# Regrouping attention rows: blocks of 32 rows of four heads, keys to the block's end, operands laid out through DRAM

## Chip, cores and metric

One NeuronCore of a Trainium2 (trn2) runs the whole kernel. The metric is the device time in microseconds of one execution; lower is better. Engines: PE is TensorE (matmuls and transposes), DVE is VectorE, ACT is ScalarE, POOL is GpSimd, SP is SyncE, which only issues DMAs.

## The reference, cut to what matters

A layer over 512 rows of width 1024. One projection gives the inputs of two attentions of 8 heads each (two groups of four heads share a key/value head); `n` is the first, with three branches that share a query, and `d` the second. Both normalise and rotate queries and keys.

```python
h = rms_norm(x, norm_gain)
proj = jnp.einsum('bsd,dc->bsc', h, w_in)
...
o_cmp, p_cmp = compressed_branch(qn, kc_cmp, vc_cmp)   # 31 compressed keys, masked by block end
o_sel = selected_branch(qn, ks_r, vs, sel_idx)         # 16 blocks wanted, 8 there are: every causal key
o_win = window_branch(qn, kw_r, vw)                    # window 512 of 512 rows: every causal key
o_nsa = g[..., 0:1] * o_cmp + g[..., 1:2] * o_sel + g[..., 2:3] * o_win
...
score = jnp.einsum('bths,bth->bts', relu(logits), wi)  # indexer
_, idx = lax.top_k(score, 128)
o_dsa = ...                                            # softmax over the 128 keys kept, causal
mixed = jnp.concatenate([o_nsa * silu(z_n), o_dsa * silu(z_d)], axis=-1)
return x + jnp.einsum('bsc,cd->bsd', mixed, w_out)
```

## The kernel before

**Tiling.** The 512 rows are four tiles of 128 (`NT = 4`). The projection runs in chunks of columns (I, C, B, Q1, Q2, D, Z0 to Z3); every product of float32 operands is three products of fp32r parts, hi·hi, hi·lo and lo·hi. ACT makes the hi part (L354), POOL most lo parts (L355). The constants, one DRAM tensor `cst`, are loaded near the start; POOL's first operation needs them.

**Attention.** A unit is one branch of one row tile i and group g, named `n{i}{g}{branch}` (1 selected, 2 window, 0 compressed) or `d{i}{g}0`. For each head h of the group the transposed queries of the tile, 128 rows, are the stationary operand, and the first 128(i + 1) keys move past them, in two products (hi and lo of the key) into one PSUM bank (`scores_of`, L964; names `s_n301` and so on, and `sc_` for the compressed branch alone). Then, in `softmax_of`:

- DVE adds the mask, multiplies by the row's norm factor `u.r` and takes the minimum, in one pass out of PSUM (L945; the page calls it CUSTOM_DVE_ANT_0);
- ACT exponentiates and sums (L947), DVE takes the reciprocals after the fourth head (L949), POOL multiplies by the gate (L951) and normalises each head (L959).

The probabilities are transposed by PE, 128 columns at a time (L999), split by ACT and DVE (L1000, L1001), and multiplied with the values (L1010). `combine` puts the four heads' outputs together. `qstack` makes the stationary queries out of the rotated ones (two transposes, L602, a copy by ACT, a subtraction by DVE, L608).

**Factors and masks.** The queries aren't normalised: `norm_of` (L562) turns sums of squares into factors `rs` by a chain of small POOL operations (`rsqrt`, L414 to L421), [row, tile × head], and the reduction applies them. The indexer's top 128 come from 16 passes MAX8 / MATCH_REPLACE of DVE (L671, L672) for each of the tiles 3, 2 and 1; POOL turns what was replaced into a mask (L674) that the `d` units of that tile use.

**Order.** `weave` mixes the attention's steps with fill work for PE (Q2, D and Z chunks, the output projection). At the end `set_order` orders every engine's instructions anew, the DMA queue of SP among them, by modelled costs and due times; `CHOICE` is one of its weights. PSUM has two banks for scores (`S`), so a third score product waits until the softmaxes of the first have read its bank. `AHEAD` is the number of units whose probabilities are kept ahead of their transposes.

Of the kernel before, what the change touches and what calls it, by code (L numbers as in the profile page):

```python
# [9 lines left out]
F32 = mybir.dt.float32  # L10
F32R = mybir.dt.float32r
# [44 lines left out]
C_VALID = C_CMASK + NT * 32  # L56
C_CCOS = C_VALID + 2
# [4 lines left out]
ARENA = 2824 + 1536 + 256 + 512 - 768 - 1024  # L62
# [6 lines left out]
TBUFS, AHEAD, LAG = 3, 3, 2  # L69
# [29 lines left out]
CHOICE = 0.25  # L99
# [208 lines left out]
def tile_hybrid_layer(ctx, tc, xT, x, ng, win, gains, peT, w1, b1, w2, wout, cst, out):  # L308
# [6 lines left out]
    psum = ctx.enter_context(tc.tile_pool(name="psum", bufs=2, space=PSUM))  # L315

# [186 lines left out]
    cmask = cs[:, C_CMASK:C_CMASK + NT * 32].rearrange("p (t c) -> p t c", t=NT)  # L503
    valid = cs[:, C_VALID:C_VALID + 1]
# [39 lines left out]
    def norm_scale(Rs_, ss):  # L544
# [7 lines left out]
        rsqrt(y, af, NT * n, div=HD, magic=MAGIC + 3 * 2.0 ** 23)  # L552
# [802 lines left out]
```

## Time and profile before

| | |
|---|---|
| median of 3 runs | 317.41 us (316.76 to 317.8) |
| profiled execution, its own time | 317.49 us |
| its span in the trace | 315.7 us |
| busy: PE, DVE, ACT, POOL | 310.4, 260.1, 243.7, 242.3 us |
| DMA moved | 30.26 MB, mean 96 GB/s |

The span runs from the first to the last instruction in the trace; the profiled execution's time has 1.8 us around it. Busy time of an engine is the time in which at least one of its instructions ran. The chain that ended last is followed backwards from the last instruction to what released each step.

### The profile page before, as it was taken

The page shows a single profiled execution, that of the slowest core. Times are in us where ns is not written, and L with a number is a line of the kernel's source. Part 1 is how long each engine was busy: PE and PEld are TensorE (multiplying, and loading weights), DVE is VectorE, ACT ScalarE, POOL GpSimd, SP SyncE. Part 2 cuts the span into 40 slices and gives each one's busy share as a digit, 9 for nine tenths or more (in the row PEclk, how much of TensorE's full clock was granted, in tenths as well). Part 3 has the DMA queues.
Part 4 walks back from the last instruction along what each step waited for, and adds up shares of the span by engine and source line. Part 5 has one row for each costly group of instructions (what it writes and reads, how often), then busy time and mean ns, then how long its engine had stood idle before and what let it go on. Part 6 is the DMA issues. An engine that isn't in the chain of part 4 may idle for free.

```text
span 315.7 us, 5949 instructions
## 1 busy us (share of the span) xinstructions
PE 310.4 (98%) x1693; PEld 261.6 (83%) x1693; DVE 260.1 (82%) x773; ACT 243.7 (77%) x791; POOL 242.3 (77%) x416
## 2 busy tenths in 40 slices
PE   8999999999999999999999999999999999999995
PEld 5988888998868888888888888888888888888885
DVE  4997523889899999999999999999998989896401
ACT  6962765989899899989999999663559997996400
POOL 2099989997995399989998988795859997757500
PEclk9999999999999999999999999999999999999999
DMA  7990455544610034100150124030426324004011
GB/s 287 395 315 3 122 154 160 163 138 123 167 48 0 2 95 132 44 1 0 30 139 1 36 69 131 3 105 28 135 67 165 104 63 137 3 0 136 0 66 66
DMA packets 14944, 30.26 MB, mean 96 GB/s; under 512 B 1792, under 2 KB 2176, under 8 KB 14912
## 3 DMA queue, kind: packets, MB, share of 16 engines
q1 hardware_dynamic: 14912, 29.90, 31.1%
q8 instruction: 13, 0.21, 0.3%
q14 instruction: 19, 0.16, 0.2%
HBM read 27.79 MB, written 2.10 MB: 95 GB/s over the span
## 4 chain that ended last, share of the span: by engine, by line
PE 90%; ACT 2%; POOL 2%; issue 2%; DMA 1%; DVE 1%; DVEq 0%; POOLq 0%; ACTq 0%
PE z L398 14%; PE out L1178 14%; PE on L1010 7%; PE B L388 7%; PE D L388 7%; PE s_n L964 6%; PE T_n L999 6%; PE Q L388 5%; PE I L477 5%; PE C L398 4%; PE s_d L964 3%; PE od L1010 3%; PE T_d L999 3%; PE qT_ps L602 1%; PE I L441 1%
## 5 line engine op out<-in xcount | busy, mean ns | idle before, releaser
L947 ACT ACTIVATE P_n<-P_n,arena 128x512 f32<-128x512 f32 (+3 forms) x64 | 36.0, 565 | 3.4 <-DVE arena L945 2.9
L945 DVE CUSTOM_DVE_ANT_0 P_n<-s_n,arena 128x512 f32<-128x512 f32 (+3 forms) x64 | 34.0, 543 | 0.4
L959 POOL TENSOR_SCALAR P_n<-P_n,arena 128x512 f32<-128x512 f32 (+3 forms) x64 | 33.1, 535 | 1.1
L964 PE MATMUL s_n<-kn,arena_r 128*128 128x512 f32 (+4 forms) x112 | 29.8, 348 | 0.5 <-DVE arena_r L608 0.5
L1001 DVE TENSOR_TENSOR ptl<-T_n,pth 128x512 fp32r<-128x512 f32 x40 | 27.4, 686 | 1.1 <-ACT pth L1000 0.5
L671 DVE MAX8 m<-scores 128x8 f32<-128x512 f32 (+2 forms) x48 | 26.6, 553 | 0.4
L672 DVE MATCH_REPLACE8 scores<-m,scores 128x512 f32<-128x512 f32 (+2 forms) x48 | 26.1, 544 | 0.1
L398 PE MATMUL z<-hThi,whi_Z 128*128 128x512 f32 x64 | 26.1, 411 | 0.0
L398 PE MATMUL z<-hTlo,whi_Z 128*128 128x512 f32 x64 | 25.3, 398 | 0.0
L398 PE MATMUL z<-hThi,wlo_Z 128*128 128x512 f32 x64 | 25.2, 397 | 0.0
L999 PE MATMUL T_n<-arena,P_n 128*128 128x128 f32 x160 | 25.2, 272 | 0.0
L1000 ACT CAST pth<-T_n 128x512 fp32r<-128x512 f32 x40 | 23.3, 581 | 2.4 <-PE T_n L999 2.3
L1178 PE MATMUL out<-whi_wo,mx 128*128 128x512 f32 (+1 forms) x72 | 24.6, 381 | 0.0
L1178 PE MATMUL out<-wohi,mx 128*128 128x512 f32 (+1 forms) x72 | 24.1, 378 | 0.0
L964 PEld LDWEIGHTS s_n<-kn,arena_r 128*128 128x128 f32 x112 | 20.0, 188 | 4.7 <-DVE arena_r L608 0.9
L999 PEld LDWEIGHTS T_n<-arena,P_n 128*128 128x128 f32 x160 | 20.0, 140 | 4.6
L355 POOL TENSOR_TENSOR wlo_Z<-raw_Z,whi_Z 128x512 fp32r<-128x512 f32 x16 | 20.5, 1297 | 3.8 <-ACT whi_Z L354 3.8
L388 PE MATMUL Q<-whi_Q,hThi 128*128 128x256 f32 (+1 forms) x64 | 22.1, 345 | 0.0
L388 PE MATMUL Q<-wlo_Q,hThi 128*128 128x256 f32 (+1 forms) x64 | 22.0, 347 | 0.0
L388 PE MATMUL Q<-whi_Q,hTlo 128*128 128x256 f32 (+1 forms) x64 | 21.7, 341 | 0.0
L355 POOL TENSOR_TENSOR w1l<-raw_w,w1h 128x512 fp32r<-128x512 f32 x16 | 20.6, 1293 | 1.2 <-DMA raw_w<-in_w_dram 1.1
L947 ACT ACTIVATE P_d<-P_d,arena 128x512 f32<-128x512 f32 (+3 forms) x32 | 17.9, 560 | 3.1 <-DVE arena L945 3.1
(262 smaller groups left out, 1105.8 us busy)
## 6 DMA issues: line engine op xcount, KB each, us to landing
raw_w<-in_w_dram SPq DMA_DIRECT2D x16, 256.0 KB, 2.9
raw_Z<-in_win_dram SPq DMA_DIRECT2D x16, 256.0 KB, 2.8
wor<-in_wout_dram SPq DMA_DIRECT2D x16, 256.0 KB, 2.8
raw_Q<-in_win_dram SPq DMA_DIRECT2D x12, 256.0 KB, 2.8
raw_D<-in_win_dram SPq DMA_DIRECT2D x8, 256.0 KB, 2.7
xres<-in_x_dram SPq DMA_DIRECT2D x8, 256.0 KB, 2.8
out_dram<-xres SPq DMA_DIRECT2D x7, 256.0 KB, 2.0
xw<-in_xT_dram SPq DMA_DIRECT2D x2, 860.0 KB, 8.0
```

Of the source, the lines that this page charges most:

```text
L355: engine.tensor_tensor(lo, raw, hi.bitcast(F32), op=ALU.subtract)
L388: nc.tensor.matmul(out_ps, a[:, k, tsl], b, start=(k == 0 and b is hi and a is hT["hi"]), stop=(k == KB - 1 and a is hT["lo"]))
L398: nc.tensor.matmul(out_ps, b[:, csl], a[:, k, :], start=(k == 0 and b is hi and a is hT["hi"]), stop=(k == KB - 1 and b is lo))
L671: nc.vector.max(m8, sc)
L945: nc.vector.tensor_tensor_reduce(P[:, h], src_, mask, u.r[:, h:h + 1], 3e38, op0=ALU.add, op1=ALU.min, accum_out=m[:, h:h + 1])
L947: nc.scalar.activation(P[:, h], P[:, h], AF.Exp, bias=m[:, h:h + 1], scale=-1.0, accum_out=l[:, h:h + 1])
L959: nc.gpsimd.tensor_scalar(P[:, hh], P[:, hh], l[:, hh:hh + 1], 1.0 if u.gate is not None else 0.5, op0=ALU.mult, op1=ALU.mult)
L964: nc.tensor.matmul(p, q[:, h, :], k[:, x], start=(x == 0), stop=(x == 1))
L999: nc.tensor.transpose(p[:, h * 128:(h + 1) * 128], u.P[:, h, j * 128:(j + 1) * 128], ident)
L1001: nc.vector.tensor_tensor(pl, p, ph.bitcast(F32), op=ALU.subtract)
L1010: nc.tensor.matmul(o, u.v[j], pp, start=(u.first and j == 0 and x == 0), stop=(end and x == 1))
L1178: nc.tensor.matmul(p, a, b[:, csl], start=(k == 0 and b is hi and a is mx[0]), stop=(k == 7 and a is mx[1]))
```

## The change

The rows of a score product are regrouped. Before, a product had 128 rows of one head; after, it has 32 rows of each of the group's four heads (block b of the tile, b = 0 to 3, in place of head h), so that only the keys up to the block's end, `keys(b)` = 128i + 32b + 32, have to move, be masked, exponentiated and normalised. Everything that is held per row has to follow that layout: [32·head + row in block, block] instead of [row, head].

- `qstack` writes the queries in blocks (the indexer keeps the old form), and `combine` reads the outputs so.
- The gates, the norm factors of q and d and the three masks go to DRAM and come back in four reads each (`by_blocks`): 8 writes and 32 reads. With two copies of the first 128 window keys (needed beside the other keys of tile 0) these are 42 more DMAs, all issued by SP.
- The mask is made by ACT (Relu with a large bias) instead of POOL.
- Transposes still take whole 128-column tiles, so DVE sets to zero the last 96 columns of blocks 0 to 2 in each of the 24 wide units (all but the compressed ones).
- A unit of kind `d` of tiles 0 and 1 no longer widens its product to 256 columns. The compressed keys share a product with the selected ones where both fit in 512 columns.
- `AHEAD` goes from 3 to 2, `CHOICE` from 0.25 to 0; POOL makes one small constant more; buffers change size.

```diff
-ARENA = 2824 + 1536 + 256 + 512 - 768 - 1024
+ARENA = 3689
...
-TBUFS, AHEAD, LAG = 3, 3, 2
+TBUFS, AHEAD, LAG = 3, 2, 2
...
-CHOICE = 0.25
+CHOICE = 0.0
...
+    trib = carve([S], BF16)
+    nc.gpsimd.memset(trib, 0.0)
+    nc.gpsimd.tensor_copy(trib[:, S - 32:], cs[:, C_TRIB:C_TRIB + 32])
...
-        rsqrt(y.rearrange("p t h -> p (t h)"), af, NT * nh, magic=MAGIC - 2.0 ** 31)
+        rsqrt(z, af, NT * 4)
+        by_blocks(y, z.rearrange("p (h t) -> p h t", t=NT), name)
...
+        if blocks:
+            pv = p[:, :256].rearrange("p (a b r) -> p a b r", a=2, b=4)
+            qv = q.rearrange("p b (a e r) -> p e a b r", a=2, e=2)
...
+    def by_blocks(dst, src_, name):
+
+        n = src_.shape[-1]
+        scr = dram.tile([128, 4 * n], F32, tag="dr_" + name, name="dr_" + name)
+        nc.sync.dma_start(scr, src_.rearrange("p h n -> p (h n)"))
+        v = scr.rearrange("(b r) (h n) -> r h b n", b=4, h=4)
+        for h in range(4):
+            nc.sync.dma_start(dst[32 * h:32 * h + 32], v[:, h])
...
-            mbias[i] = b8.tile([128, n], BF16, tag=f"masks{i}", name=f"masks{i}")
-            nc.gpsimd.tensor_scalar(mbias[i], sc, -2e38, NEG, op0=ALU.is_gt, op1=ALU.mult)
+                nc.vector.match_replace(sc, m8, sc, -3e30)
+            mk = b8.tile([128, n], BF16, tag=f"masks{i}", name=f"masks{i}")
+
+            nc.scalar.activation(mk, sc, AF.Relu, bias=big)
+            mbias[i] = dram.tile([128, n], BF16, tag=f"dr_mask{i}", name=f"dr_mask{i}")
+            nc.sync.dma_start(mbias[i], mk)
...
+            if b:
+                for k in kn:
+                    nc.sync.dma_start(k[:, :, K_WIN0:K_CMP].bitcast(F32), k[:, :, 0:128].bitcast(F32))
...
+        P, m, l = u.P[:, b, :n], u.m, u.l
+        nc.vector.tensor_tensor_reduce(P, src_, mask, u.r[:, b:b + 1], 3e38, op0=ALU.add, op1=ALU.min,
+                                       accum_out=m[:, b:b + 1])
+        if b == 0 and u.P.shape[-1] > 32:
+
+            nc.vector.memset(u.P[:, 0:3, u.P.shape[-1] - 96:], 0.0)
+        nc.scalar.activation(P, P, AF.Exp, bias=m[:, b:b + 1], scale=-1.0, accum_out=l[:, b:b + 1])
...
-                for hh in range(4):
-                    nc.gpsimd.tensor_scalar(P[:, hh], P[:, hh], l[:, hh:hh + 1], 1.0 if u.gate is not None else 0.5,
+                for bb in range(4):
+                    Pb = u.P[:, bb, :128 * u.i + 32 * bb + 32]
+                    nc.gpsimd.tensor_scalar(Pb, Pb, l[:, bb:bb + 1], 1.0 if u.gate is not None else 0.5,
...
-    def scores_of(p, q, h, k):
-        for x in range(2):
-            nc.tensor.matmul(p, q[:, h, :], k[:, x], start=(x == 0), stop=(x == 1))
-
-    def softmax_steps(k, parts):
-
-        u = parts[0][0]
-        n = k.shape[-1]
-        for h in range(4):
-            p = ps("S", "s_" + u.name)[:, :n]
-            scores_of(p, u.q[0], h, k)
-            for v, cols, mask in parts:
-                softmax_of(v, h, p[:, cols], mask)
-            yield 2 * COST * n
-
-    def compressed_steps(u, k, mask):
-        p = ps("S", "sc_" + u.name)
-        for h in range(4):
-            scores_of(p[:, 32 * h:32 * h + 32], u.q[0], h, k)
-        for h in range(4):
-            softmax_of(u, h, p[:, 32 * h:32 * h + 32], mask)
-        yield 0.86
+    def softmax_steps(q, products):
+
+        for b in range(4):
+            for k, parts in products(b):
+                n = k.shape[-1]
+                p = ps("S", "s_" + parts[0][0].name)[:, :n]
+                for x in range(2):
+                    nc.tensor.matmul(p, q[0][:, b], k[:, x], start=(x == 0), stop=(x == 1))
+                for v, cols, mask in parts:
+                    softmax_of(v, b, p[:, cols], mask)
+                yield 2 * COST * max(n, 256)
...
+        keys = lambda b: 128 * i + 32 * b + 32
+        causal = lambda b: trib[:, S - keys(b):]
...
+            if g == 0 and i:
+
+                mm = work.tile([128, 4, n], BF16, tag="mm", name=f"mm{i}", bufs=2)
+                v = mbias[i].rearrange("(b r) n -> r b n", b=4)
+                for h in range(4):
+                    nc.sync.dma_start(mm[32 * h:32 * h + 32], v)
+                ST["mm", i] = mm
+            u.S = lambda: softmax_steps(q, lambda b: [
+                (ST["kdi"][:, g, :, :keys(b)], [(u, slice(0, keys(b)), ST["mm", i][:, b, :keys(b)] if i else causal(b))])])
...
-            us.S = lambda: softmax_steps(k[:, :, w0:K_SEL + n], [sel(n + 32), win_, cmp(n)])
+            us.S = lambda: softmax_steps(q, lambda b: [
+                (k[:, :, K_WIN0:K_SEL + 128], [sel(b, 160), win_(b), cmp(b, 128)])])
         else:
-            uw.S = lambda: softmax_steps(k[:, :, w0:S], [win_])
-            if i < 3:
-                us.S = lambda: softmax_steps(k[:, :, K_CMP:K_SEL + n], [sel(32), cmp(0)])
-            else:
-                us.S = lambda: softmax_steps(k[:, :, K_SEL:], [sel(0)])
-                uc.S = lambda: compressed_steps(uc, k[:, :, K_CMP:K_SEL], cmask[:, i, :])
+            uw.S = lambda: softmax_steps(q, lambda b: [(k[:, :, 0:keys(b)], [win_(b)])])
+            us.S = lambda: softmax_steps(q, lambda b: [
+                (k[:, :, K_CMP:K_SEL + keys(b)], [sel(b, 32), cmp(b, 0)])] if keys(b) + 32 <= 512 else [
+                (k[:, :, K_SEL:], [sel(b, 0)]), (k[:, :, K_CMP:K_SEL], [cmp(b, 0)])])
```

How the order changes, at three places. The first is PE at the first score products (`s_n301`, tile 3, group 0, selected branch; `Q2_*` are projection products, `hid1` the compression's). Before:

```order
L964 MATMUL s_n301_1489<-kn0_385,arena_r_71 128x512 [waits DVE_49]
L964 MATMUL s_n301_1489<-kn0_385,arena_r_71 128x512
L388 MATMUL Q2_1_1466<-wlo_Q22_1087,hThi_72 128x512
L388 MATMUL Q2_1_1466<-whi_Q22_1086,hTlo_73 128x512
L388 MATMUL Q2_1_1466<-whi_Q23_1096,hThi_72 128x512
L388 MATMUL Q2_1_1466<-wlo_Q23_1097,hThi_72 128x512
L757 MATMUL hid1_1321<-arena_70,scr_1320 128x64 x2
L964 MATMUL s_n301_1498<-kn0_385,arena_r_71 128x512 [waits DVE_49,PE_49]
L964 MATMUL s_n301_1498<-kn0_385,arena_r_71 128x512
```

and after, where the lines are L1010 for score products, L390 for projections:

```order
L790 MATMUL hid1_1345<-arena_72,scr_1344 128x64 [waits DVE_49]
L790 MATMUL hid1_1345<-arena_72,scr_1344 128x64
L1010 MATMUL s_n301_1528<-kn0_397,arena_r_73 128x448 [waits DVE_49]
L1010 MATMUL s_n301_1528<-kn0_397,arena_r_73 128x448 [waits Activation_49]
L1010 MATMUL s_n301_1540<-kn0_397,arena_r_73 128x480 x2
L390 MATMUL Q2_2_1615<-whi_Q20_1083,hThi_74 128x512 [waits DVE_49,PE_49]
L390 MATMUL Q2_2_1615<-wlo_Q20_1084,hThi_74 128x512
L390 MATMUL Q2_2_1615<-whi_Q20_1083,hTlo_75 128x512
L390 MATMUL Q2_2_1615<-whi_Q20_1083,hThi_74 128x512
L390 MATMUL Q2_2_1615<-wlo_Q20_1084,hThi_74 128x512
L390 MATMUL Q2_2_1615<-whi_Q20_1083,hTlo_75 128x512
L1010 MATMUL s_n301_1550<-kn0_397,arena_r_73 128x512 [waits PE_49]
```

Before, the first score products stand between the Q2 products of row tile 1, one head at a time, two of four heads in these rows. Now all of Q2's tile 1 comes before them, blocks 0 and 1 follow at once with 448 and 480 columns (the 32 compressed keys are in them), and block 2 waits for the bank behind six products of tile 2.

The second is DVE at the first softmax. Before (L945 the reduction, L672 an indexer pass, ISA without shape names the readout of the minimum):

```order
L672 MATCH_REPLACE scores3_558<-m8_597,scores3_558 128x512 [waits DVE_49]
L945 ISA P_n301_1492,arena_70<-s_n301_1489,arena_70 128x512 [waits PE_49,Pool_49]
L945 ISA arena_70 128x1
L945 ISA P_n301_1492,arena_70<-s_n301_1498,arena_70 128x512 [waits PE_49]
L945 ISA arena_70 128x1
L671 MAX m8_597<-scores3_558 128x8 [waits DVE_49]
```

and after (L982 the reduction, L986 the zeroing):

```order
L701 MATCH_REPLACE scores_391<-m8_608,scores_391 128x512 [waits DVE_49]
L982 ISA P_n301_1531,arena_72<-s_n301_1528,arena_72 128x416 [waits DMAHW5_49,DMAHW4_49,DMAHW6_49,DMAHW3_49,PE_49]
L982 ISA arena_72 128x1
L986 MEMSET P_n301_1531 128x3x96
L982 ISA arena_72<-s_n301_1528,arena_72 128x32
L982 ISA arena_72 128x1
L982 ISA P_n301_1531,arena_72<-s_n301_1540,arena_72 128x448 [waits DVE_49,PE_49]
L982 ISA arena_72 128x1
L982 ISA arena_72<-s_n301_1540,arena_72 128x32
L982 ISA arena_72 128x1
```

The first reduction waited for PE and POOL, and now waits for PE and for four DMA lanes; each block has two reductions, 416 or 448 wide and 32 wide, and the zeroing stands behind the first.

The third is SP's queue, where the factors of q0 go out and come back. Before, chunk D's weights stand alone:

```order
L350 DMA raw_D2_1370<-in_win_dram 128x512 [waits DMAHW5_49,Pool_49]
L350 DMA raw_D3_1374<-in_win_dram 128x512 [waits DMAHW6_49,Pool_49]
L350 DMA raw_D4_1380<-in_win_dram 128x512 [waits DMAHW7_49,Pool_49]
L350 DMA raw_D5_1384<-in_win_dram 128x512 [waits DMAHW0_49,Pool_49]
L350 DMA raw_D6_1390<-in_win_dram 128x512 [waits DMAHW1_49,Pool_49]
L350 DMA raw_D7_1394<-in_win_dram 128x512 [waits DMAHW2_49,Pool_49]
```

and after (L894 the copies of window keys, L657 the write, L660 the four reads):

```order
L352 DMA raw_D3_1413<-in_win_dram 128x512 [waits DMAHW3_49,Pool_49]
L894 DMA kn0_397<-kn0_397 128x2x128 [waits DMAHW0_49,DVE_49,Activation_49]
L894 DMA kn1_398<-kn1_398 128x2x128 [waits DVE_49,PE_49,Activation_49]
L657 DMA dr_q0_1338<-nz_1319 128x16 [waits Pool_49]
L660 DMA arena_72<-dr_q0_1338 32x4x4 [waits DMAHW2_49]
L660 DMA arena_72<-dr_q0_1338 32x4x4 [waits DMAHW4_49]
L660 DMA arena_72<-dr_q0_1338 32x4x4 [waits DMAHW5_49]
L660 DMA arena_72<-dr_q0_1338 32x4x4 [waits DMAHW6_49]
L352 DMA raw_D4_1419<-in_win_dram 128x512 [waits DMAHW7_49,Pool_49]
L352 DMA raw_D5_1423<-in_win_dram 128x512 [waits DMAHW0_49,Pool_49]
L352 DMA raw_D6_1429<-in_win_dram 128x512 [waits DMAHW1_49,Pool_49]
```

Two copies, a write that waits for POOL and four reads that wait for the write now stand between the weights D3 and D4.

## Rows read from the trace of the kernel before

**Rows 1.** Page: busy times of the engines; shares of the chain that ended last.
```profile
PE 310.4 (98%) x1693; PEld 261.6 (83%) x1693; DVE 260.1 (82%) x773; ACT 243.7 (77%) x791; POOL 242.3 (77%) x416
...
PE 90%; ACT 2%; POOL 2%; issue 2%; DMA 1%; DVE 1%; DVEq 0%; POOLq 0%; ACTq 0%
```

**Rows 2.** Windows: stretch, span, then each engine's busy time, clock, DMA share, GB/s.
```profile
100.00:220.00 120.00, 120.00 (x636) 100.37 (x635) 116.26 (x364) 105.18 (x367) 103.05 (x194) 1.00 0.19 54
220.00:300.00 80.00, 80.00 (x430) 67.06 (x429) 67.24 (x213) 61.90 (x186) 61.15 (x92) 1.00 0.27 80
```

**Rows 3.** Timeline of PE: start, us, engine, line, operation, out<-in, shape, count.
```profile
137.85 0.40 PE L964 MATMUL s_n<-kn,arena_r 128*128 128x256 f32 x2
138.09 0.39 PE L388 MATMUL D<-whi_D,hThi 128*128 128x512 f32 x1
138.32 0.40 PE L388 MATMUL D<-wlo_D,hThi 128*128 128x512 f32 x1
```

**Rows 4.** Chain that ended last, 90 to 108: start, us, what.
```profile
91.74 0.73 PE s_n L964 x2
...
97.09 0.47 PE s_n L964 x2
...
106.13 0.80 PE sc_n L964 x8
```

**Rows 5.** Timeline of PE, 5 to 9.
```profile
5.75 0.76 PE L477 MATMUL I<-whi_I,hTlo 128*128 128x92 f32 x4
6.35 0.75 PE L477 MATMUL I<-wlo_I,hThi 128*128 128x92 f32 x4
```

**Rows 6.** Groups of DVE by form: count, busy us, mean ns, idle before.
```profile
L945 DVE CUSTOM_DVE_ANT_0 P_n<-s_n,arena 128x512 f32<-128x512 f32 x16 | 11.6, 744 | 0.1
...
L945 DVE CUSTOM_DVE_ANT_0 P_n<-s_n,arena 128x128 f32<-128x128 f32 x16 | 5.0, 347 | 0.0
...
L437 DVE MEMSET arena<- 128x448 uint32 x1 | 0.4, 432 | 0.9 <-PEq L1343 0.9
```

**Rows 7.** Timeline of DVE, 22.0 to 23.2: a chain of dependent small operations.
```profile
22.16 0.17 DVE L429 TENSOR_TENSOR vx_ps<-vx_ps,arena 128x4 f32<-128x4 f32 x1
22.36 0.17 DVE L430 TENSOR_TENSOR vx_ps<-vx_ps,nwa 128x4 f32<-128x4 f32 x1
```

**Rows 8.** Timeline of POOL, 85 to 95.
```profile
85.31 1.30 POOL L355 TENSOR_TENSOR wlo_Q<-raw_Q,whi_Q 128x512 fp32r<-128x512 f32 x1
...
87.96 0.23 POOL L562 TENSOR_TENSOR naf<-ss_q,arena 128x16 f32<-128x16 f32 x1
...
93.99 0.22 POOL L421 TENSOR_TENSOR arena<-nwt,arena 128x16 f32<-128x16 f32 x1
```

**Rows 9.** Timeline of DVE, 94 to 97.
```profile
95.64 0.74 DVE L945 CUSTOM_DVE_ANT_0 P_n<-s_n,arena 128x512 f32<-128x512 f32 x1
```

**Rows 10.** DMA issues: count, KB each, median us from issue to landing.
```profile
raw_w<-in_w_dram SPq DMA_DIRECT2D x16, 256.0 KB, 2.9
...
arena<-in_cst_dram SPq DMA_DIRECT2D x1, 513.0 KB, 11.4
...
out_dram<-xres SPq DMA_DIRECT2D x2, 128.0 KB, 1.9
```

**Rows 11.** Timeline of SP's queue, 0 to 20.
```profile
4.66 0.46 SPq L498 DMA_DIRECT2D arena<-in_cst_dram  x1
```

**Rows 12.** Timeline of POOL and DVE, 170 to 171.
```profile
170.45 0.21 POOL L421 TENSOR_TENSOR arena<-nwt,arena 128x16 f32<-128x16 f32 x1
...
170.88 0.75 DVE L945 CUSTOM_DVE_ANT_0 P_d<-s_d,masks,arena 128x512 f32<-128x512 f32 x1
```

**Rows 13.** Timeline of POOL, 14 to 40.
```profile
16.23 3.03 POOL L502 CAST arena<-arena 128x128 bf16<-128x128 f32 x1 [13.80 <-DMA arena<-in_cst_dram]
...
32.42 5.05 POOL L355 TENSOR_TENSOR wlo_B<-raw_B,whi_B 128x512 fp32r<-128x512 f32 x4
```

**Rows 14.** Timeline of PE, 37 to 39.
```profile
37.90 0.40 PE L388 MATMUL B<-wlo_B,hThi 128*128 128x512 f32 x1
```

More of the change, by code (lines that the diff above doesn't have):

```diff
@@ L642, in tile_hybrid_layer @@
     kix = b8.tile([128, 2, S], F32R, tag="kix", name="kix")
-    mbias = {0: tri[:, S - 128:S]}
+    mbias = {}
+    scores = b8.tile([128, 1152], F32, tag="scores", name="scores")
+    big = carve([1], F32)
+    nc.gpsimd.memset(big, 2.5e30)
     def indexer():
@@ L653, in indexer @@
             n = 128 * (i + 1)
-            q, nq = nq, qstack(ridx, i - 1) if i > 1 else None
+            q, nq = nq, qstack(ridx, i - 1, False) if i > 1 else None
             yield 0.2
-            sc = b8.tile([128, n], F32, tag=f"scores{i}", name=f"scores{i}")
+            s0 = 64 * i * (i + 1) - 128
+            sc = scores[:, s0:s0 + n]
             for h in range(4):
@@ L686, in tile_hybrid_layer @@
     vcs = vall[:, NT * 4:]
-    kn = [b8.tile([128, 2, 2 * S + 32], F32R, tag=f"kn{g}", name=f"kn{g}") for g in range(2)]
-    K_CMP, K_SEL = S, S + 32
+    kn = [b8.tile([128, 2, 2 * S + 160], F32R, tag=f"kn{g}", name=f"kn{g}") for g in range(2)]
+    K_WIN0, K_CMP, K_SEL = S, S + 128, S + 160
     diag = carve([4, 128], BF16)
@@ L857, in kb_stack @@
         for b in range(2):
-            kstack([two(k, slice(0, S) if b else slice(K_SEL, None)) for k in kn], ST["kb_raw"][b], 0, 2, back=bool(b))
+            kstack([two(k, slice(0, S) if b else slice(K_SEL, None)) for k in kn], ST["kb_raw"][b], 0, 2)
+            if b:
+                for k in kn:
+                    nc.sync.dma_start(k[:, :, K_WIN0:K_CMP].bitcast(F32), k[:, :, 0:128].bitcast(F32))
             yield 0.4
@@ L877, in tile_hybrid_layer @@
     Rs = {}
-    rs = {(key, g): carve([NT, 4], F32) for key in "qd" for g in range(2)}
+    rs = {(key, g): carve([4, NT], F32) for key in "qd" for g in range(2)}
     def queries(name, key, j, gs, nxt, after=(), rest=(None, None, None)):
@@ L930, in tile_hybrid_layer, with softmax_of @@
     turn, turn_c = [0], [0]
-    def softmax_of(u, h, src_, mask):
+    def softmax_of(u, b, src_, mask):
         n = src_.shape[-1]
-        if h == 0:
-            if n == 32:
+        if b == 0:
+            if u.b == 0 and u.kind == "n":
                 u.P = pcs[:, turn_c[0] % (AHEAD + 1)]
@@ L988, in transposed @@
         pl = work.tile([128, 512], F32R, tag="ptl", name="ptl", bufs=TBUFS)
-        if u.b == 2:
+        if u.b == 0 and u.kind == "n":
             nc.tensor.transpose(p[:, :128], u.P.rearrange("p h c -> p (h c)"), ident)
@@ L1032, in combine @@
     def combine(o, dst):
-        ov = o.rearrange("p (a b q) -> p a b q", a=2, b=2)
-        for b in range(2):
-            d = dst[b * 64:(b + 1) * 64]
-            nc.scalar.copy(d, ov[0:64, :, b, :])
-            nc.vector.tensor_tensor(d, ov[64:128, :, b, :], d, op=ALU.add)
-    on = b8.tile([128, NT, 2, 2, 128], F32, tag="on", name="on")
+        ov = o.rearrange("p (b a e r) -> p e a b r", b=4, a=2, e=2)
+        for e in range(2):
+            d = dst[e * 64:(e + 1) * 64].rearrange("p a (b r) -> p a b r", b=4)
+            nc.scalar.copy(d, ov[0:64, e])
+            nc.vector.tensor_tensor(d, ov[64:128, e], d, op=ALU.add)
+    on_ = b8.tile([128, NT + 2, 2, 128], F32, tag="on", name="on")
+    on = {(i, g): on_[:, NT + i % 2 if g else i] for i in range(NT) for g in range(2)}
     od = {}
@@ L1049, in units_of @@
             u = Unit()
-            u.b = 2 if kind == "n" and b == 0 else 0
+            u.b, u.i = b, i
             u.name = f"{kind}{i}{g}{b}"
             u.q, u.o, u.done = q, o, done
-            u.dst = on[:, i, g] if kind == "n" else None
+            u.dst = on[i, g] if kind == "n" else None
             u.first = b == order[0]
@@ L1152, in mix @@
     def mix(half, i, g):
-        o = on[:, i, g] if half == 0 else od[f"{i}{g}"]
+        o = on[i, g] if half == 0 else od[f"{i}{g}"]
         m = b8.tile([128, 2, 2, 128], F32R, tag=f"mx{half}{g}", name="mx", bufs=2)
```

89 lines of the change are left out of this document (46 added, 43 removed).

## Prediction

> **What bounds the kernel now.** I read the page first: TensorE (PE) is busy 98% of the span, and 90% of the chain that ended last is its own work [rows 1]. So the time is the sum of what PE issues, plus what it waits. Then the stretches: PE is busy all 120.00 us of 100 to 220 and all 80.00 of 220 to 300, but in the first VectorE (DVE) is busy 116.26 too, only 3.74 us short of full; in the second it has 12.76 us to spare [rows 2]. ScalarE and GpSimd (POOL) have 15 to 17 us to spare in the first and are not at their end. A saving on PE therefore counts in full only if DVE, almost as full for 120 us, doesn't grow, and no new wait stops PE's stream.
>
> A busy time of PE overstates an instruction, since matmuls overlap; the price is the distance from one start to the next. Two 256-wide score products take 138.09 − 137.85 = 0.24 us, 0.12 each; the 512-wide product behind them takes 0.23 [rows 3]. From these two: about 5 ns + 0.445 ns for each column. Eight 32-wide ones take 0.80, 0.10 each [rows 4]; there is a floor, which I set at 0.11 us.
>
> **Score products (what the change is for).** I counted widths in both programs. Before: 192 products, 65,536 columns (48 of 512, 16 of 416, 32 of 384, 32 of 288, 48 of 256, 16 of 32). Changed: 180 products, 55,808 columns: a block's keys end at the block, 48 columns fewer on average, and the one-row-tile units of kind d are no longer padded to 256. By the law with its floor: 31.58 us before, 27.78 after, **−3.8 us**. The stationary side keeps its 128 columns, so weight loads don't shrink. Whether a width under 256 keeps the law matters, since 44 of the new products have widths between 64 and 224, where the floor already decides. The nearest row is a group of one 92-wide and three 348-wide products of the same type, 6.35 − 5.75 = 0.60 us [rows 5]; three 348-wide ones are 0.48 by the law, which leaves 0.12 for the 92-wide one: no penalty. If all 52 narrower than 256 cost as much as 256 columns, 0.12, the saving would be 0.5 smaller; so between −3.3 and −4.0 (all 52 at the 0.10 of the 32-wide ones).
>
> A 512-wide product is 0.23 us here, nearly twice a 256-wide one [rows 3]; so the cost goes with the columns and hardly with the count. The Trainium skill (TensorE: Matmul & The Clock Gate, Back-to-back issue gap) gives another law for a stream: 81 ns for 128 columns, 131 ns for 512, that is, a large fixed part and a flat slope. By it the scores would be an estimated 20.9 us before and 18.8 after, −2.1 instead of −3.8; the trace disagrees with its 131 ns (rival E).
>
> **DVE.** The 96 softmaxes' reductions become 48 columns narrower: 0.744 us at 512 and 0.347 at 128 is 1.03 ns a column, so 96 × 48 × 1.03 = −4.8 us [rows 6]. Each of the 24 wide units now also zeroes 3 × 96 columns of its probabilities. No such row exists; the nearest is a memset of 448 columns, 0.432 us [rows 6], so 288 columns lie between 0.28 (in proportion) and 0.43. I take 0.30, nearer to proportion: 24 × 0.30 = +7.2 us. DVE's balance is **+2.4 us** (1.9 to 5.5). Block 1's reduction writes over zeroed columns and so waits for the memset; dependent small operations start 0.20 apart though each lasts 0.17 [rows 7], so a wait of about 0.1 each time, up to 24 × 0.12 = 2.9 us if nothing else is queued between. I cost this at nothing in the sum: the work that hides it is the 3.74 + 12.76 us of free DVE [rows 2], and the order has fill work for PE beside it. Without that cover it is rival D.
>
> ScalarE and POOL: exponentials and normalisations become narrower as well; three mask operations go from POOL to ScalarE. Both engines end up with less or about the same, and neither was full: nothing.
>
> **First softmax behind a round trip through DRAM.** The norm factors of q0 now go out to DRAM and come back as four reads, before DVE's first softmax, which stands in DVE's queue with the indexer and the ropes behind it. Before: the last split for Q2 on POOL begins at 85.31, the factor chain runs from 87.96 to 93.99 + 0.22 = 94.2 [rows 8], and DVE takes the first softmax at 95.64 [rows 9]. After: behind that split POOL has one small operation and one 0.75 us rope product instead of two, so the chain begins near 87.5; 26 small operations of 0.2 us (some of them of the compressed keys) stand up to its last: 92.6. To this the trip adds: the nearest rows are the smallest write, 1.9 us to landing, and reads of 2.9 [rows 10], with 0.46 us for an issue on SP [rows 11]. Lower bound 1.9 + 1.9 = 3.8, upper 2.9 + 4 × 0.46 + 2.9 = 7.6; taken 1.9 + 3 × 0.46 + 1.9 = 5.2, since these transfers are small and the write row is the nearest. First softmax at 97.8. The third score product needs the bank that block 0's softmaxes free: 416 columns 0.64 and 32 columns 0.25 by the slope of [rows 6], zeroing 0.30, so 99.0. PE would be there at 96.0: up to it both orders hold the same PE work (90.6 us by the law before, 90.5 after), and before it stood at 97.09 with 0.95 us lost, since 91.74 to 97.09 is 5.35 us for 4.4 us of work [rows 4]. So 3.0 us of waiting instead of 0.95: +2.05; bounds by the trip's bounds +0.7 to +4.5. Some may be cheaper, as PE has 16.3 us of work between Q1's last product and the first score product instead of 9.8, and ScalarE's sums may finish earlier by it. I take **+1.9**.
>
> **The other trips.** Of gates, q1, d1 and three masks the results are used long after. The critical one is d0: its last factor operation ends at 170.45 + 0.22, and the first softmax of kind d follows at 170.88 [rows 12], with no slack. But the changed order has 16.8 us of PE work between D's last product and that unit's first product, before 11.6: 5.2 us more, as much as the trip. Cost nothing; if the cover is gone, one more trip less its cover, at most 2.4 us. SP's queue takes 42 more transfers of 0.46 us, 19 us of issue, spread over 200 us; a weight chunk queued behind a trip comes up to 2 us later, ahead of which several chunks are buffered: nothing.
>
> **The start.** The constants' transfer is issued at 4.66 [rows 11] and takes 11.4 us [rows 10]; POOL's first work waits for it at 16.23, and what it has to do then lasts until the split that ends at 32.42 + 5.05 = 37.47 [rows 13], which feeds the B product at 37.90 [rows 14]. A 512 KB weight transfer now stands ahead of the constants, and POOL gets one small cast more. Late by 0 to 1.3 us (slack 0.4); I take **+0.4**.
>
> **Sum.** −3.8 + 1.9 + 0.4 = −1.5. On the profiled run's 317.49 us (0.08 above the median of 317.41) that is 316.0, and 315.9 on the median: **315.9 us**. A run of this kernel can be told from no change beyond 0.3%, about 0.95 us.
>
> **Rivals.**
> A, forecast: 314.6 to 316.4.
> B, the trip is hidden: PE's extra 6.5 us of work ahead of the first scores means that all is ready when PE comes. Then −3.8 + 0.4, possibly less the 0.95 lost before: 313.1 to 314.2. For it: the moved work; against: the factor chain is paced by POOL, full up to there.
> C, given back: the trip at its upper end and the start late, −3.8 + 3.0 to 4.5 + 0.4 to 1.3: 317.0 to 318.3. For it: five serial transfers on one queue with waits on their lanes.
> D, slower: DVE becomes the bound in 100 to 220. Its 116.26 us grow by 2.4 and by 2.9 of waits to 121.6, 1.6 over the stretch; PE's saving there (about half, 1.9) is lost, the rest and the two delays stay: 317.4 + 1.6 − 1.9 + 2.3 = 319.4. It decides once the added DVE time passes the 3.74 us of idle. For it: [rows 2]; against: DVE is free from 220 on, and the fixed order can place PE's fill work against it.
> E, the saving doesn't follow the columns: a product had a fixed part as large as half of a 512-wide one, 0.12 us, and the slope were half. Then 192 × 0.12 + 65,536 × 0.00022 = 37.5 becomes 180 × 0.12 + 55,808 × 0.00022 = 33.9, −3.6 in place of −3.8 and 316.1; by the flatter law named above, −2.1 and about 317.6. [Rows 3] bear out neither: a 256-wide one is half of a 512-wide one. Chance 0.02.
> That products under 256 columns run at a quarter of the rate would make +4.8 out of −3.8; [rows 5] exclude it.
> That the change doesn't shorten the products is excluded by the count.
>
> **Numbers.** A 0.43, B 0.15, C 0.22, D 0.18, E 0.02. The likeliest is A, 315.9. Its own range is 314.6 to 316.4; eight in ten takes in B's better part, C and half of D: 313.1 to 319.2. Faster by over 0.3% (under 316.45): A and B, with half of E, 0.59; within: C, less its end, and half of E, 0.22; slower: D and that end, 0.19.
>
> **What would show it.** Score products of 416 columns starting 0.19 us apart; a DVE row of 24 memsets at 0.28 to 0.43 us; the first softmax waiting for a DMA, near 97.8; a PE gap of about 3 us around 96 to 99 and no other over 1 us; DVE idle in 100 to 220 above 1 us. It is wrong if DVE's idle there falls to nothing while PE shows gaps behind softmaxes, if kind d's first unit stalls on its trip, or if the splits of the B chunks make PE wait near 38.

## The result, and the profile after

The changed kernel takes 316.03 us (median of 20 runs, 314.86 to 316.81), the kernel before, timed beside it, 317.9. The ratio is 0.994 with a 95% interval of 0.9928 to 0.9952, that is 1.5 to 2.3 us less; forecast were 1.5 less and 315.9. The profiled execution is an unlucky one: 316.42 us, against 317.49 for the profiled one of before, so the two traces differ by only 1.1 us (spans 314.6 and 315.7).

The page of the changed kernel, busy times and the chain that ended last, to hold against [rows 1]:

```profile
PE 306.6 (97%) x1681; PEld 258.9 (82%) x1681; DVE 261.1 (83%) x797; ACT 242.3 (77%) x794; POOL 234.1 (74%) x416
...
PE 81%; ACT 7%; DMA 4%; POOL 3%; issue 2%; DVE 1%; SPq 1%; POOLq 0%; DVEq 0%
```
PE's work fell by 3.8 us, as counted; but the span fell by 1.1. PE's idle time rose from 5.3 us (315.7 − 310.4) to 8.0. The view of waits for PE names it (us in all, times, longest):

```profile
PE idx L689 <- DVE scores L695: 2.1, 2, 1.3
PE I L443 <- DVE arena L445: 1.4, 1, 1.4
PE qT_ps L611 <- issue: 0.8, 1, 0.8
PE s_n L1010 <- DVE arena_r L621: 0.5, 1, 0.5
```
In the trace before, the same view has the wait at the start (1.4) and the one of the first score product (0.5), and otherwise only 0.3 us at `kT_ps`:

```profile
PE I L441 <- DVE arena L443: 1.4, 1, 1.4
PE s_n L964 <- DVE arena_r L608: 0.5, 1, 0.5
PE kT_ps L584 <- ACT kb_raw L557: 0.3, 1, 0.3
```
New are 2.1 us in which products of the indexer (`idx`) wait for VectorE's `scores`, and 0.8 ahead of the first query transposes (`qT_ps`) of kind d. So 2.1 + 0.8 − 0.3 = 2.6 of the 2.7 us are named. On PE's timeline (the bracket is the idle time ahead of the row):

```profile
62.35 0.73 PE L689 MATMUL idx<-kix,arena_r 128*128 128x512 f32 x2 [1.29 <-DVE scores L695]
...
71.09 0.61 PE L689 MATMUL idx<-kix,arena_r 128*128 128x384 f32 x2 [0.78 <-DVE scores L695]
...
96.28 1.12 PE L1010 MATMUL s_n<-kn,arena_r 128*128 128x448 f32 x4 [0.54 <-DVE arena_r L621]
...
98.64 0.62 PE L1010 MATMUL s_n<-kn,arena_r 128*128 128x512 f32 x2
...
102.78 0.53 PE L1010 MATMUL s_n<-kn,arena_r 128*128 128x416 f32 x2
103.15 0.39 PE L390 MATMUL Q<-whi_Q,hThi 128*128 128x512 f32 x1
...
169.33 0.41 PE L611 MATMUL qT_ps<-arena,R_d 128*128 128x128 f32 x2 [0.78 <-issue]
```
At 96.28 PE waits for VectorE's query subtraction as it did before at 91.74; ahead of the third score product, at 98.64, where I had forecast a gap of 3 us, there is none. Two 416-wide products take 103.15 − 102.78 = 0.37 us, where the law has 0.38.

Why do the indexer's products wait? SP's queue shows it (start, time to issue all, count):

```profile
51.22 0.33 SPq L657 DMA_DIRECT2D dr_gate<-arena  x1
53.08 1.28 SPq L660 DMA_DIRECT2D arena<-dr_gate  x3
54.41 0.43 SPq L352 DMA_DIRECT2D raw_w<-in_w_dram  x1
54.88 0.43 SPq L660 DMA_DIRECT2D arena<-dr_gate  x1
55.41 10.67 SPq L352 DMA_DIRECT2D raw_w<-in_w_dram  x7
...
92.22 0.60 SPq L657 DMA_DIRECT2D dr_q<-nz  x1
93.92 1.76 SPq L660 DMA_DIRECT2D arena<-dr_q  x4
```
The gates' write goes out at 51.22, the first read can be issued only at 53.08, when the write has landed, and the eight weight transfers of the compression (`raw_w`) stand behind and between the reads. Before, they began at 52.68:

```profile
52.68 11.54 SPq L350 DMA_DIRECT2D raw_w<-in_w_dram  x8
```
Now the first leaves at 54.41 and the rest from 55.41; the last has been issued at 66.08 instead of 64.22. ScalarE, whose instructions run in order, waits for them with the indexer's relu behind:

```profile
57.44 0.62 ACT L356 CAST w1h<-raw_w 128x512 fp32r<-128x512 f32 x1 [1.01 <-DMA raw_w<-in_w_dram]
...
59.33 0.62 ACT L356 CAST w1h<-raw_w 128x512 fp32r<-128x512 f32 x1 [0.58 <-DMA raw_w<-in_w_dram]
...
68.46 0.62 ACT L356 CAST w1h<-raw_w 128x512 fp32r<-128x512 f32 x1 [1.24 <-DMA raw_w<-in_w_dram]
```
The first two stand ahead of PE's wait at 62, the third ahead of the one at 71. VectorE adds up after the relu, and PE waits for VectorE to free the bank. That is the theory: a trip through DRAM costs where it stands in SP's queue ahead of weights that are due soon, and not where its own result is used. The rival: the planner's new order around the indexer makes the gaps, and the queue has no part in it.

VectorE and its zeroings, with the first stretch of [rows 2] again:

```profile
L986 DVE MEMSET P_n<- 128x288 f32 x16 | 4.8, 298 | 0.1
...
L986 DVE MEMSET P_d<- 128x288 f32 x8 | 2.4, 298 | 0.1
```
```profile
100.00:220.00 120.00, 119.22 (x634) 99.67 (x633) 116.10 (x378) 105.29 (x368) 97.78 (x189) 1.00 0.23 64
```
24 zeroings of 0.298 us are 7.2 us, as forecast; VectorE ends at 116.10 of 120, no fuller than before.

### The profile page after: what moved, and what is told of

It reads as the page before. It is cut to its first block, busy times and chain, and to the rows that moved or that the text cites. A ratio compares the mean times of both kernels' runs of the same rounds, so it can differ in the third digit from the quotient of the medians.

```text
span 314.6 us, 6043 instructions
## 1 busy us (share of the span) xinstructions
PE 306.6 (97%) x1681; PEld 258.9 (82%) x1681; DVE 261.1 (83%) x797; ACT 242.3 (77%) x794; POOL 234.1 (74%) x416
## 4 chain that ended last, share of the span: by engine, by line
PE 81%; ACT 7%; DMA 4%; POOL 3%; issue 2%; DVE 1%; SPq 1%; POOLq 0%; DVEq 0%
PE out L1219 14%; PE z L400 14%; PE D L390 7%; PE on L1040 7%; PE s_n L1010 6%; PE T_n L1029 6%; PE Q L390 5%; PE I L479 5%; DMA raw_w<-in_w_dram 4%; PE C L400 3%; PE od L1040 3%; PE T_d L1029 3%; PE s_d L1010 3%; POOL w1l L357 2%; PE I L443 1%
## 5 line engine op out<-in xcount | busy, mean ns | idle before, releaser
L987 ACT ACTIVATE P_n<-P_n,arena 128x416 f32<-128x416 f32 (+9 forms) x64 | 33.5, 525 | 3.3 <-DVE arena L982 2.8
L1000 POOL TENSOR_SCALAR P_n<-P_n,arena 128x416 f32<-128x416 f32 (+7 forms) x64 | 30.4, 493 | 1.1
L982 DVE CUSTOM_DVE_ANT_0 P_n<-s_n,arena 128x416 f32<-128x416 f32 (+9 forms) x64 | 30.3, 489 | 0.5
L1010 PE MATMUL s_n<-kn,arena_r 128*128 128x288 f32 (+12 forms) x116 | 28.3, 328 | 0.5 <-DVE arena_r L621 0.5
L1029 PE MATMUL T_n<-arena,P_n 128*128 128x128 f32 x160 | 26.9, 272 | 0.0
L1010 PEld LDWEIGHTS s_n<-kn,arena_r 128*128 128x128 f32 x116 | 20.7, 188 | 4.6 <-DVE arena_r L621 0.7
L1219 PE MATMUL out<-whi_wo,mx 128*128 128x512 f32 (+1 forms) x72 | 23.6, 379 | 0.0
L390 PE MATMUL Q<-whi_Q,hThi 128*128 128x256 f32 (+1 forms) x64 | 22.4, 349 | 0.0
L390 PE MATMUL Q<-whi_Q,hTlo 128*128 128x256 f32 (+1 forms) x64 | 22.2, 347 | 0.0
L390 PE MATMUL Q<-wlo_Q,hThi 128*128 128x256 f32 (+1 forms) x64 | 21.8, 340 | 0.0
L1040 PE MATMUL on<-ptl,arena_r 128*128 128x512 f32 x48 | 20.0, 417 | 0.0
```

The source lines that it names most:

```text
L390: nc.tensor.matmul(out_ps, a[:, k, tsl], b, start=(k == 0 and b is hi and a is hT["hi"]), stop=(k == KB - 1 and a is hT["lo"]))
L982: nc.vector.tensor_tensor_reduce(P, src_, mask, u.r[:, b:b + 1], 3e38, op0=ALU.add, op1=ALU.min, accum_out=m[:, b:b + 1])
L987: nc.scalar.activation(P, P, AF.Exp, bias=m[:, b:b + 1], scale=-1.0, accum_out=l[:, b:b + 1])
L1000: nc.gpsimd.tensor_scalar(Pb, Pb, l[:, bb:bb + 1], 1.0 if u.gate is not None else 0.5, op0=ALU.mult, op1=ALU.mult)
L1010: nc.tensor.matmul(p, q[0][:, b], k[:, x], start=(x == 0), stop=(x == 1))
L1029: nc.tensor.transpose(p[:, h * 128:(h + 1) * 128], u.P[:, h, j * 128:(j + 1) * 128], ident)
```

## Experiments

Ratios are to the kernel before, each with its 95% interval; beside the changed kernel's 0.994 (± 0.0012) a difference of 0.001 is 0.32 us, and one of less than 0.002 (0.003 where the run's own interval is the widest) is not told from nothing. `set_order` plans anew whenever the program changes, and another plan alone may move the time. In the runs named "same order" every engine's instruction order is that of the changed kernel; only what is named differs.

**The gates' trip left out.**
```diff
-    nc.gpsimd.tensor_scalar(gate, gate, 0.25, 0.25, op0=ALU.mult, op1=ALU.add)
+    nc.gpsimd.tensor_scalar(gate2, gate, 0.25, 0.25, op0=ALU.mult, op1=ALU.add)
-    by_blocks(gate2..., gate..., "gate")
```


> The changed kernel without the gates' trip through DRAM: the gates stay in the old layout, so they are applied to the wrong rows; all other work is the same. Queue theory: the trip's reads stand in SP's queue ahead of eight weight transfers of the compression, these land late, ScalarE waits for them with the indexer's relu behind it, and PE loses 2.4 us at 62 and 71. Without it both gaps (1.45 and 0.94) go, and the time falls by 1.5 to 2.5 us against the changed kernel, to about 314.0. Rival: the gaps come from the new order of VectorE, ScalarE and PE around the indexer; then they stay and the time changes by less than 0.5 us.

314.36 us, ratio 0.9898 (0.9878 to 0.9918): 1.3 us less, a little under the 1.5 expected at least. Both waits at the indexer are gone from its trace. By itself this doesn't part the theories, as the plan is new.

**The trip later in the plan**, two ways: behind the last `raw_w`, and behind the last Q2 weight (emitted with q0's factors; the planner is told that the write depends on that weight).
```diff
+        if named(k, "dr_gate"):
+            before[k].add(last)     # last "raw_w", in the second kernel last "raw_Q2"
```


> The changed kernel with the gates' trip kept, but emitted with the norm factors of q0 and not let into SP's queue before the last of the compression's weights. Queue theory: like the run without the trip, 1.5 to 2.5 us faster than the changed kernel, unless the trip now delays the Q2 weights among which it stands (then half of it, 0.7 to 1.2). Rival: less than 0.5 us.

> As gate_gap, but planned anew on all engines with the rule that the gates' trip comes behind the last Q2 weight. Queue theory: the same gain, 1.4 to 2.2 us, give or take the 0.5 us of another plan: ratio 0.986 to 0.991.

314.55 us, 0.9907 (0.9889 to 0.9926), and 314.29 us, 0.9889 (0.9871 to 0.9908): 1.0 and 1.6 us less than the changed kernel. In the first the write and the reads stand among Q2's weights. That behind Q2 is better than among Q2 is what the queue theory says, but the intervals overlap. The second plan turned out to be the changed kernel's on PE, VectorE, ScalarE and GpSimd: operations and tiles follow each other there as in its trace, and only SP's queue differs. So its 1.6 us aren't another plan's either.

**Same order, the trip moved behind the compression's weights.**
```diff
+    trip, last = at("dr_gate"), at("raw_w")[-1]
+    sp[:] = [k for k in sp if k not in trip]
+    sp[sp.index(last) + 1:sp.index(last) + 1] = trip
```


> The changed kernel with the same planned order on every engine; only in SP's queue the five transfers of the gates stand behind the eight weight transfers of the compression instead of among and ahead of them. Queue theory: weights land some 2 us earlier, the PE gaps at 62 and 71 (2.4 us together) shrink to under 0.8, time 1.2 to 2.4 us below the changed kernel (ratio to before 0.987 to 0.990). Rival (the order of PE around the indexer makes the gaps, whatever the queue does): both gaps stay, ratio 0.994.

319.89 us, 1.0059 (1.0042 to 1.0077): 3.8 us slower than the changed kernel, against both expectations. The view of waits for PE, and SP's queue:

```profile
PE hid L815 <- ACT uT L801: 3.2, 1, 3.2
...
PE idx L694 <- DVE scores L700: 0.2, 1, 0.2
```
```profile
50.76 14.34 SPq L357 DMA_DIRECT2D raw_w<-in_w_dram  x8
65.14 0.43 SPq L662 DMA_DIRECT2D dr_gate<-arena  x1
67.89 1.75 SPq L665 DMA_DIRECT2D arena<-dr_gate  x4
69.75 11.20 SPq L357 DMA_DIRECT2D raw_Q<-in_win_dram  x8
```
The weights of the compression now go from 50.76 on, and the waits at the indexer have shrunk from 2.1 to 0.2 us with PE's order untouched: the rival falls. But the trip now stands ahead of Q2's weights, which leave at 69.75; its write took 2.75 us until the first read could go. ScalarE waits for them, and this time a copy for the compression's second stage (`uT`) is behind it, for which PE waits 3.2 us:

```profile
72.60 0.62 ACT L361 CAST whi_Q<-raw_Q 128x512 fp32r<-128x512 f32 x1 [3.70 <-DMA raw_Q<-in_win_dram]
```
So the theory held and my choice of place did not: I had not asked what stands behind the trip in the new place. And the loss is more than the wait. PE's clock in that trace, windows of 2 us (the third number from the end is the granted clock):

```profile
74.00:76.00 2.00, 1.70 (x9) 1.63 (x10) 2.00 (x6) 2.00 (x11) 1.30 (x3) 0.67 0.34 71
76.00:78.00 2.00, 2.00 (x10) 1.66 (x10) 2.00 (x7) 0.67 (x4) 2.00 (x3) 0.50 0.39 120
78.00:80.00 2.00, 2.00 (x19) 2.00 (x19) 1.97 (x6) 0.90 (x2) 1.43 (x5) 0.98 0.68 193
```
Two of the products in between:

```profile
75.73 0.41 PE L395 MATMUL Q<-whi_Q,hThi 128*128 128x256 f32 x1
75.95 0.41 PE L395 MATMUL Q<-wlo_Q,hThi 128*128 128x256 f32 x1
```
After 3.2 us without work the granted clock is 0.67, then 0.50, the lower level of 1.2 GHz, and back at 0.98 from 78 on; products of 256 columns start 0.22 us apart in between and 0.12 after. From 74.9 to 78.1 half of the time is lost to that level, 1.6 us, beside the 3.2 of the wait. Eleven of this kernel's twelve executions have a mean granted clock of 0.989 to 0.994 and take 319.07 to 320.43 us; the one at 0.999 takes 317.2, still more than the changed kernel's 316.03 (how long PE waited in that one is not on record).

**Same order, the trip where the queue is idle**: behind the first four weights of chunk D. Same edit with `sp.index(first kn copy)` as the place.

> The changed kernel with the same planned order on every engine; in SP's queue the gates' five transfers stand behind the first four weight transfers of chunk D and ahead of the two key copies, where the queue had nothing to issue from 84.7 to 88.8. Queue theory: nothing urgent is behind them there, so the gaps at the indexer shrink as they did when the trip stood behind the compression's weights, the new gap of 3.4 us at 74 doesn't come, and the time is 1.4 to 2.2 us below the changed kernel: ratio to before 0.987 to 0.990. Rival (any later place delays something else as much): not below 0.993.

314.44 us, 0.9893 (0.9874 to 0.9912): 1.5 us less than the changed kernel.

```profile
PE I L448 <- DVE arena L450: 1.4, 1, 1.4
PE qT_ps L616 <- issue: 0.8, 1, 0.8
PE s_n L1015 <- DVE arena_r L626: 0.5, 1, 0.5
```
```profile
82.46 0.57 SPq L662 DMA_DIRECT2D dr_gate<-arena  x1
85.09 1.77 SPq L665 DMA_DIRECT2D arena<-dr_gate  x4
```
The waits at the indexer are gone, and none takes their place. A write and four reads, the same in number and size and in an order otherwise the same, cost 1.5 us, 5.3 us (1.0059 against 0.9893, the lost clock included) or, beside the kernel without the trip (0.9898, with a plan of its own), nothing that can be told, by what stands behind them.

**The factors' trips left out**, and **same order, trips made but not waited for**:
```diff
-        by_blocks(y, z.rearrange("p (h t) -> p h t", t=NT), name)      # left out
...
-            u.r = rs["q" if kind == "n" else "d", g][:, :, i]         # made, not waited for
+            u.r = nz[...].rearrange("p (h t) -> p h t", t=NT)[:, :, i]
```


> The changed kernel with the norm factors of q and d used in the old layout (wrong rows), their four trips left out, the gates' and masks' trips kept. By the prediction the q0 trip costs 1.9 us at the first softmax, so 1.9 us faster than the changed kernel, near 314.1. By the trace of the changed kernel the trip ends before PE needs it: same time within 0.5 us, with the gaps at 62 and 71 still there.

> The changed kernel with the same planned order on every engine and all transfers made, but the reductions take the norm factors in the old layout (wrong rows) and wait for none of the four trips of q and d. If the round trip costs at the first softmax as predicted, 1.9 us less, ratio 0.988. If it is covered by PE's moved work, the same as the changed kernel within 0.4 us, ratio 0.993 to 0.995; then the 1.3 us that the run without these trips gained came from its new order.

314.41 us, 0.99 (0.9875 to 0.9926), and 315.2 us, 0.9924 (0.9907 to 0.9941). The first, planned anew, has another order at the indexer, without the two gaps, though the gates' trip stands in the same place: so how much a late weight costs depends on the order too. The second decides on the round trip: 0.5 ± 0.7 us less than the changed kernel, where 1.9 were forecast. Its waits:

```profile
PE idx L699 <- DVE scores L705: 0.9, 1, 0.9
...
PE s_n L1022 <- DVE arena_r L631: 0.5, 1, 0.5
```
The wait of the first score product is 0.5 with and without the trip. What little it gained stands at the indexer (0.9 in place of 2.1), ahead of any use of the factors. The run with small zeroings further down, which does wait for the factors and differs in nothing up to there, has 1.2:

```profile
PE idx L691 <- DVE scores L697: 1.2, 2, 0.7
```
So with the gates' trip in its place the wait at the indexer is 2.1, 1.2 or 0.9 us from one execution to another, and the profiled one of the changed kernel shows the longest.

**Score products over all keys again**, softmaxes as changed:
```diff
-                (ST["kdi"][:, g, :, :keys(b)], [(u,
+                (ST["kdi"][:, g, :, :max(n, 256)], [(u,
-            uw.S = lambda: softmax_steps(q, lambda b: [(k[:, :, 0:keys(b)], [win_(b)])])
+            uw.S = lambda: softmax_steps(q, lambda b: [(k[:, :, 0:n], [win_(b)])])
```
(and likewise for the selected branch.) 

> The changed kernel with every score product over all keys of the tile, as before the change (and 256 for kind d's small ones); softmaxes still read only the block's keys, results unchanged. By the columns: PE has 3.4 to 3.8 us more work and the time rises by that, to 319.5 to 319.9. If the saving didn't follow the columns (rival E) it rises by about 2. If VectorE were the bound (rival D) by less than 1.

318.9 us, 1.0044 (1.0029 to 1.0059): 3.3 ± 0.6 us more than the changed kernel, a little under the 3.4 to 3.8 expected. The order is planned anew here, and the trace has neither the waits at the indexer nor the one ahead of kind d's query transposes: PE's busy time is 4.5 us above the changed kernel's (311.1 against 306.6), its idle time 1.8 below (317.3 − 311.1 = 6.2 against 8.0). So the 3.3 us are the widths' price less what the other plan gave back, and by these two traces the narrower products are worth 3.3 us or rather more. With the wide products the change is 1.4 us slower than before.

**Zeroing**, smaller in the same order, and moved to GpSimd in a new plan:
```diff
-            nc.vector.memset(u.P[:, 0:3, u.P.shape[-1] - 96:], 0.0)
+            nc.vector.memset(u.P[:, 0:3, z:], 0.0)      # z: last column in 15 of 24 units
...
+            nc.gpsimd.memset(u.P[:, 0:3, u.P.shape[-1] - 96:], 0.0)
```


> The changed kernel with the same planned order, but 15 of the 24 zeroings on VectorE write 1 column in place of 96 for each of three blocks (the rest of the columns keep old values, so probabilities there are wrong). VectorE loses 15 x 0.24 = 3.6 us of work. If that work is covered as the prediction says: same as the changed kernel within 0.4 us. If VectorE decides in 100 to 220 (rival D): 1 to 3 us faster.

> The changed kernel with the 24 zeroings on GpSimd instead of VectorE (planned anew). VectorE loses 24 x 0.30 = 7.2 us of work. If VectorE is no bound: within 0.7 us of the changed kernel, which is what another plan may do; if it decides in 100 to 220: 1 to 3 us faster.

315.46 us, 0.9931 (0.9914 to 0.9947), and 315.03 us, 0.9913 (0.9885 to 0.994). With the order kept, 3.6 us less work of VectorE is worth 0.3 ± 0.7 us; in 100 to 220 it is then busy 115.00 us, and PE's stretch is the same:

```profile
100.00:220.00 120.00, 119.22 (x634) 99.84 (x633) 115.00 (x378) 105.19 (x364) 98.19 (x190) 1.00 0.24 65
```
On GpSimd the gain of 0.9 ± 0.9 us is at the edge of what can be told.

**The planner's constants alone, in the kernel before** (`CHOICE` 0, `AHEAD` 2). 

> The kernel before with only the changed constants of the planner and buffers: one unit fewer kept ahead, and no weight on switching rows. If the gain is the narrower products' the time stays within 1 us of before; if it came from the new order, it falls by about 2 us. A wait of the kind at the indexer could make it slower by 1 to 2 us.

317.34 us, 0.999 (0.9975 to 1.0004): in the kernel before, the constants alone gain nothing that can be told. In the changed kernel the old ones weren't tried.

**The best of it**: trip behind Q2 and zeroing on GpSimd. 

> The changed kernel with both: the gates' trip behind the last Q2 weight, and the zeroings on GpSimd, planned anew. If the gates' place is what was lost and the zeroing is covered: as gate_later, 314.3 us, ratio 0.987 to 0.991. If the two gains add (zero_pool's 0.9913 came from VectorE and not from its other plan): 0.984 to 0.987.

313.98 us, 0.9883 (0.9864 to 0.9901), 1.8 us less than the changed kernel; not told from the later trip alone (0.9889).

## Why the prediction came out right

The sum was right, two of its three terms weren't, and a term put at nothing cost as much as the trip was to cost. That the total came out within 0.4 us of the forecast is luck: two misses of about 2 us cancel.

**Score products, −3.8: right.** 3.8 us of PE's busy time; 3.3 ± 0.6 on the clock when undone, in another plan. The flatter law of rival E, 2.1 us, lies outside that interval; its first form, −3.6, isn't told from the forecast by the time, only by [rows 3] and the pair of 416-wide products. (The forecast's better bound, all 52 narrow products at 0.10, is −4.2 when added up again, not −4.0; rival C's own terms reach 319.4, not 318.3. Neither changes the argument.)

**First softmax behind the trip, +1.9: wrong, it cost nothing.** The trip itself was sized well: the chain's last operation ended at 91.8 (forecast 92.6), the first softmax began at 97.25 (97.8). But it began there because VectorE came from an indexer pass, with no idle time ahead of it: the sign that I had named, a first softmax waiting for a DMA, didn't come. POOL from its start to this chain, and VectorE at the first softmax:

```profile
17.98 2.07 POOL L504 CAST arena<-arena 128x128 bf16<-128x128 f32 x1 [14.93 <-DMA arena<-in_cst_dram]
...
33.28 5.05 POOL L357 TENSOR_TENSOR wlo_B<-raw_B,whi_B 128x512 fp32r<-128x512 f32 x4
...
91.34 0.31 POOL L537 TENSOR_TENSOR kscr<-rk,rk 64x64 f32<-64x64 f32 x1 [1.32 <-DVE rk L536]
91.61 0.21 POOL L423 TENSOR_TENSOR nz<-nwt,nz 128x16 f32<-128x16 f32 x1
```
```profile
96.65 0.68 DVE L701 MATCH_REPLACE8 scores<-m,scores 128x512 f32<-128x512 f32 x1
97.25 0.64 DVE L982 CUSTOM_DVE_ANT_0 P_n<-s_n,arena 128x416 f32<-128x416 f32 x1
...
98.12 0.13 DVE L982 CUSTOM_DVE_ANT_0 arena<-s_n,arena 128x32 f32<-128x32 f32 x1
```
The step that failed is the distance between two times that I worked out apart: the chain by POOL's work alone, with the first softmax at 97.8, and PE by the order before, "PE would be there at 96.0", so that PE had to wait. In the changed kernel PE came at 98.64, since 2.1 us had been lost at the indexer and 0.5 at the first score product, and block 0's bank was free at 98.25. Where nothing is lost at the indexer, in the trace with the trip in the idle place, PE comes at 96.30, near the forecast, and still doesn't wait, since the chain has moved along (q0's write leaves at 89.92 instead of 92.22):

```profile
94.92 0.65 DVE L987 CUSTOM_DVE_ANT_0 P_n<-s_n,arena 128x416 f32<-128x416 f32 x1
```
```profile
96.30 0.62 PE L1015 MATMUL s_n<-kn,arena_r 128*128 128x512 f32 x2
```
PE comes 1.39 us after the first softmax begins in the one trace and 1.38 in the other; forecast was 1.8 ahead of it. So that the chain ended about when I had said is luck: it was late by the loss at the indexer, which I had not forecast. The chain isn't paced by POOL alone, which I had held against rival B: its last operation stands in POOL's order behind a product that waits 1.32 us for VectorE. Chain and PE wait for the same things further up, and the 6.5 us of PE work that the order put ahead of the scores covers the trip: the mechanism of rival B, to which I gave 0.15 (that the trip costs nothing is measured; that this work is its cover is a reading, since no run takes the work away). Nor does the trace before bear out the 0.95 us lost here: no wait of PE is named there, and from 91.74 to the third score product it has 4 score, 12 Q2 and 10 compression products, 4.8 us by the law and not 4.4.

**The other trips, "a weight chunk queued behind a trip comes up to 2 us later, ahead of which several chunks are buffered: nothing": wrong.** The delay was sized right (1.7 us for the first of the eight, 1.9 for the last), the cover wasn't looked up: I took buffers to be ahead, and ScalarE was waiting for these very weights. The gates' trip cost 2.1 us in the trace, 1.5 ± 0.7 in the time of the run that moves it.

**Start, +0.4: nothing.** The constants came 1.75 us later (17.98 against 16.23), the split behind them ended at 38.33 instead of 37.47 [rows 13], and PE was busy all of 20 to 40: so it had that much slack.

**VectorE: right.** 7.2 us of zeroing were covered (its busy time rose by 1.0 us in all, 260.1 to 261.1, where +2.4 was forecast); rival D falls by the run with small zeroings.

**Kind d's first unit:** its trip didn't stall, but PE waits 0.8 us ahead of its query transposes at 169.33. In all five traces with this order that row starts 0.10 us after the end of ScalarE's copy of d's keys; why it should wait for that copy stays open. In the run with zeroing on GpSimd, planned anew, the wait doesn't occur.

So −3.8 + 0 + 0 + 2.1 + 0.8 − 0.3 = −1.2 on the traces (measured 1.1): one wait named in the wrong place, and another of the same size denied. With the 1.5 us of the timed runs in place of this trace's 2.1 the sum is −1.8, against 1.9 between the medians; with the trip in the idle place it is −3.3, and that run is 3.4 us below before.

## What to carry to other kernels

A transfer through DRAM that is off the critical path still stands in its queue: list what is queued behind its wait, and which engine, in order, waits for that; put it where the queue has nothing due. When a result comes later, ask whether the engine that uses it comes later too by the same cause, before the difference is called a wait. And with a planner in the kernel, test a suspicion with the order held fixed, since a new plan brings waits of its own and takes others away: here both waits at the indexer went when the factors' trips were left out, though the gates' trip stood ahead of the same weights.

## What the runs showed of the hardware

A wait of 3.2 us on PE was followed by some 3 us at half the granted clock, the waits of 1.29 and 0.78 us in the changed kernel by none: there the mean clock is 1.0.

In the changed kernel's trace the gates' reads, 12 KB each, landed in 1.8 us and the queries' factors, 2 KB, in 1.7 (medians), hardly less than the two writes of 128 KB to `out_dram`, 1.8. From a small write's issue to the first read's it took 1.70 us behind two copies of 128 KB (92.22 to 93.92) and 2.75 behind eight weight transfers of 256 KB (65.14 to 67.89).
